# Two experts side by side on the column halves of TensorE, with plain transposes, one scatter for both, and second-layer weights loaded two rows to a packet

## The chip, the cores and the metric

The kernel runs on one core of one Trainium2 chip. The metric is the device time of one execution in microseconds, as the median of several runs. Everything is computed in float32; the dense products outside the experts split each operand into two parts, the expert products don't.

## What is computed

The reference is one block with retention, dilated attention and a mixture of experts, followed by a second block of two layers, all for 256 tokens of width 1024. The change touches the mixture of experts alone. Each token goes to 4 of 32 experts; an expert is two matrix products with a clamped SwiGLU between them:

```python
logits = (xf @ w_router + b_router)
top_val, top_idx = lax.top_k(logits, TOP_K)
gates = jax.nn.softmax(top_val, axis=-1)
...
u = xb @ w1[e] + b1[e]                       # w1[e]: 1024 x 2048
glu = jnp.minimum(u[:, ::2], SWIGLU_LIMIT)
lin = jnp.clip(u[:, 1::2], -SWIGLU_LIMIT, SWIGLU_LIMIT)
a = glu * jax.nn.sigmoid(SWIGLU_ALPHA * glu) * (lin + 1.0)
return a @ w2[e] + b2[e]                     # w2[e]: 1024 x 1024
...
y = y.at[row_tok].add(yb * row_gate[:, None])
```

## The kernel before

**The program.** First come the dense layers of the first block, then the router (lines 868 to 940), then the experts (to line 1160), then the second block. The expert stage lasts from some 369 to 1375 us of the profiled execution, half of the whole.

**Tokens in slots.** Each expert has 64 slots. `gather` (L965) picks the tokens of four experts at a time with one-hot matrices and leaves them transposed in the tile `hg`: hidden dimension on the partitions, 64 slots per expert along the free axis. Experts with more than 64 tokens are made up for in `past_slots`, a branch that is skipped when there are none.

**First product, `chunk(e)`.** The tokens are the stationary operand (128 rows, 64 columns), the weights stream through as 512 columns. 64 columns fill half of the array, so two products run beside each other, on its two column halves, into partitions 0 to 63 and 64 to 127 of one PSUM bank (`halves`, L995). Before the change the two halves are the odd and the even blocks of 128 hidden rows of the same expert: each half holds half of the sum. Each float32 product shows as two instructions in the trace.

**Merge and transpose.** The four banks are copied to `us` by ScalarE and VectorE (L320, L1014). Then 16 products per expert (L1019) with `jh`, two identity matrices of 64 on top of each other, add the two halves and transpose them in one step; the columns are read with a step of two, so that the two interleaved parts, gated and linear, come apart. Bias, clamp, activation and the last product follow on VectorE and ScalarE (L1022 to L1027) into `apk`.

**Second product, `second(e)`.** It runs the same way (L995 again, into banks of tag b), with the halves as even and odd blocks of the middle dimension. The result `ys` therefore again holds half sums in its two halves. For each pair of experts the scatter (L1059) multiplies by `spread`, a matrix with the gate of each token at its slot, twice, so that the halves are added on the way, and VectorE adds the result to `acc` (L1064). `spread_pair` builds two such matrices per token block and pair (L985, L987).

**Order of the work.** `jobs` puts the first product of expert e + 1 ahead of the second product of expert e, so that the activation of e is covered. A scheduler may move instructions within that.

**Weights.** `W.plan` is one list of tiles of 1 MB in the order of use; they are issued on SP's queue in that order (`load_next`, L143). During the expert stage they lie in two rings of six buffers, `raw` and `more`, which take turns in blocks of six; the first 16 tiles are loaded ahead, four of them into other buffers. A load waits until the tile that had its buffer has been used. A first-layer tile is 128 rows of 8 KB, one to a partition. A second-layer tile is 256 rows of 4 KB: partition p gets the rows p and p + 128, two packets of 4 KB. From 16 tiles before the end of the stage on, only the ring `raw` is used, and the tiles of the second block follow in it; those are split into two parts by ScalarE and VectorE (L172, L173).

Of the kernel before, what the change touches and what calls it, by code (L numbers as in the profile page):

```python
# [36 lines left out]
def constants():  # L37
# [5 lines left out]
    c["halves"] = np.concatenate([np.eye(64), np.eye(64)], axis=0)  # L43
    c["before"] = (i[:, None] < i[None, :])
    c["slots"] = np.tile(np.arange(64) + 1, (P, 2))
# [162 lines left out]
def body(tc, A, out, offs, dbg):  # L208
# [75 lines left out]
    jobs = [("c", 0)] + [j for e in range(31) for j in (("c", e + 1), ("h", e))] + [("h", 31)]  # L284
    for kind, e in jobs:
        for k in range(0, 8, 1 if kind == "c" else 2):
            W.add((kind, e, k), kpf(w1[e], 0, 2 * D, k, 1) if kind == "c" else kpf(w2[e], 0, D, k, 2), True)
# [659 lines left out]
    apk = pe.tile([P, 2, 8, SLOTS], F32, name="apk")  # L947
    b1T = pe.tile([P, 2, 8, 32], F32, name="b1T")
    us_ = pa.tile([P, 4, 512], F32, name="us", tag="x1")
    jh = con("halves")  # L950
    spread, ys = {}, {}
# [20 lines left out]
    for g in range(2):  # L972
        for k in range(8):
            f0 = k % 4 * 256 + g
            PE.transpose(b[:, (g * 8 + k) * 32:(g * 8 + k + 1) * 32], b1w[k // 4][:, f0:f0 + 255:2], ident[:32, :32])
    copy_s(b1T.rearrange("p g k e -> p (g k e)"), b)

    def spread_pair(p_):

        od = pe.tile([P, 2, 2, P], F32, name="od")  # L980
        b = bank("b").rearrange("p (e b t) -> p e b t", e=2, b=2)
        for i in range(2):
            for tb in range(2):
# [4 lines left out]
        spread[p_] = pe.tile([P, 2, 2, P], F32, name="spread")  # L988
        copy_s(spread[p_], b)
# [7 lines left out]
    lo_, hi_ = slice(0, SLOTS), slice(SLOTS, P)  # L997

    def chunk(e, ahead):
        u = [bank("a") for _ in range(4)]  # L1000
        last = []
        for k in range(0, 8, 2):
            for g, d in ahead[k // 2:k // 2 + 1]:
# [6 lines left out]
        eb = [bank("b").rearrange("p (k s) -> p k s", k=8) for _ in range(2)]  # L1010
        us = us_ if e == 0 else pa.tile([P, 4, 512], F32, name="us", tag="x1")
# [540 lines left out]
```

## Time and profile before

| | us |
|---|---|
| median of 3 runs (2001.44 to 2003.26) | 2002.59 |
| the profiled execution | 2001.25 |
| its span, first to last instruction | 1999.3 |
| TensorE busy in the span | 1961.2 (98%) |
| VectorE busy | 819.3 (41%) |
| ScalarE busy | 597.2 (30%) |
| transfers on SP's queue | 583.07 MB, 76.7% of 16 engines' span |

Engines: PE is TensorE's products, PEld its weight loads, DVE is VectorE, ACT ScalarE, SP the queue that issues the loads. Where a row of windows lists busy times without names, they stand in the order PE, PEld, DVE, ACT, POOL. "Granted clock" is the share of TensorE's full clock. A matmul's end is modelled, so the busy share of TensorE is an upper bound, and what ends the waits of others tells more. The transfer share is the mean busy share of the 16 transfer engines. Bank tags a and b are two sets of four PSUM banks.

### The profile page before, as it was taken

To read this page: it belongs to the slowest core of one execution; us is meant where nothing else is said; L and a number is where in the kernel's file an instruction comes from. 1 tells how busy PE (TensorE), PEld (TensorE's weight loads), DVE (VectorE), ACT (ScalarE), POOL (GpSimd) and SP (SyncE) were. 2 spreads that over 40 slices of the span, in tenths; PEclk is the share of its full clock that TensorE was granted. 3 is DMA by queue.
4 is the path that set the end of the run, shared out by engine and by line. 5 is a ranking of instruction groups with operands and counts; after the bars stand their busy time and mean duration, and the time that the engine had idled before them with its cause. 6 is when DMAs were issued, how large, how long until landed. Compare 5 with 4: busy or idle time off the path is not lost. (4 is left out here: it accounts for less than half of the span.)

```text
span 1999.3 us, 25851 instructions
## 1 busy us (share of the span) xinstructions
PE 1961.2 (98%) x10812; PEld 1279.2 (64%) x10812; DVE 819.3 (41%) x1324; ACT 597.2 (30%) x900; POOL 2.6 (0%) x7
## 2 busy tenths in 40 slices
PE   7999999899999999999999999999999999999998
PEld 6899987544444444444444443436879998979997
DVE  6687577311211112121121111325665446556455
ACT  4535543211111111111111111103634444645443
POOL 0000000000000000000000000000000000000000
PEclk9999999999999999999999999999999999999999
DMA  9777576898999999999999999989536555336550
GB/s 361 258 245 235 179 265 243 325 394 333 414 386 400 417 379 416 396 402 418 382 416 391 404 417 382 376 351 375 198 127 211 188 180 181 126 105 207 180 183 22
DMA packets 203293, 593.26 MB, mean 297 GB/s; under 512 B 10587, under 2 KB 95158, under 8 KB 170402
## 3 DMA queue, kind: packets, MB, share of 16 engines
q1 hardware_dynamic: 196792, 583.07, 76.7%
q10 hardware_dynamic: 6378, 8.47, 1.3%
q8 instruction: 87, 1.43, 0.3%
q14 instruction: 36, 0.29, 0.0%
HBM read 590.44 MB, written 1.07 MB: 296 GB/s over the span
## 5 line engine op out<-in xcount | busy, mean ns | idle before, releaser
L173 DVE TENSOR_TENSOR wlo<-raw,whi 128x1024 fp32r<-128x1024 f32 x286 | 345.3, 1221 | 248.7 <-ACT whi L172 246.7
L172 ACT ACTIVATE whi<-raw 128x1024 fp32r<-128x1024 f32 x286 | 298.1, 1058 | 340.6 <-issue 101.9
L995 PE MATMUL bank_a<-more,hg 128*64 128x512 f32 x1440 | 318.5, 594 | 0.0
L995 PE MATMUL bank_b<-raw,apk 128*64 128x512 f32 x1024 | 264.7, 601 | 0.0
L995 PEld LDWEIGHTS bank_a<-more,hg 128*64 128x64 f32 x1440 | 101.7, 137 | 193.5 <-issue 190.7
L1014 DVE COPY us<-bank_a 128x512 f32<-128x512 f32 x64 | 44.2, 692 | 396.4 <-PE bank_a L995 396.4
L366 PE MATMUL bank_b<-xh,whi 128*128 128x256 f32 x640 | 181.2, 283 | 0.0
L368 PE MATMUL bank_b<-xh,wlo 128*128 128x256 f32 x640 | 181.0, 283 | 0.0
L367 PE MATMUL bank_b<-xl,whi 128*128 128x256 f32 x640 | 181.0, 283 | 0.0
L1019 PEld LDWEIGHTS bank_b<-cm,us 128*128 128x128 f32 x1024 | 127.0, 196 | 68.1 <-issue 41.4
L995 PEld LDWEIGHTS bank_b<-raw,apk 128*64 128x64 f32 x1024 | 70.0, 136 | 118.7 <-issue 97.6
L995 PE MATMUL bank_a<-raw,hg 128*64 128x512 f32 x608 | 141.8, 597 | 0.1
L1019 PE MATMUL bank_b<-cm,us 128*128 128x64 f32 x1024 | 138.4, 285 | 0.7 <-ACT us L320 0.7
L320 ACT ACTIVATE us<-bank_a 128x512 f32<-128x512 f32 x64 | 38.1, 597 | 289.0 <-PE bank_a L995 289.0
L366 PEld LDWEIGHTS bank_b<-xh,whi 128*128 128x128 f32 x640 | 122.7, 192 | 0.7
L367 PEld LDWEIGHTS bank_b<-xl,whi 128*128 128x128 f32 x640 | 122.6, 192 | 0.7
L368 PEld LDWEIGHTS bank_b<-xh,wlo 128*128 128x128 f32 x640 | 122.7, 192 | 0.0
L1059 PE MATMUL bank_b<-y,spread 128*128 128x512 f32 x256 | 122.4, 611 | 0.0
L995 PEld LDWEIGHTS bank_a<-raw,hg 128*64 128x64 f32 x608 | 42.2, 136 | 84.9 <-issue 77.2
L1059 PEld LDWEIGHTS bank_b<-y,spread 128*128 128x128 f32 x256 | 44.8, 189 | 76.7 <-issue 55.0
L1024 ACT ACTIVATE glu<-glu 128x512 f32<-128x512 f32 x32 | 20.2, 630 | 243.0 <-DVE glu L1023 243.0
L1064 DVE TENSOR_TENSOR acc<-bank_b,acc 128x512 f32<-128x512 f32 x52 | 36.0, 692 | 134.1 <-PE bank_b L1059 134.1
(389 smaller groups left out, 2896.2 us busy)
## 6 DMA issues: line engine op xcount, KB each, us to landing
raw<-in_w_mlp SPq DMA_DIRECT2D x204, 1024.0 KB, 10.4
more<-in_w_mlp SPq DMA_DIRECT2D x180, 1024.0 KB, 11.1
raw<-in_w_ffn_in SPq DMA_DIRECT2D x44, 1024.0 KB, 5.2
raw<-in_w_in SPq DMA_DIRECT2D x38, 1024.0 KB, 7.8
raw<-in_w_ada SPq DMA_DIRECT2D x24, 1024.0 KB, 7.6
raw<-in_w_ffn_out SPq DMA_DIRECT2D x22, 1024.0 KB, 5.0
raw<-in_b_w_in SPq DMA_DIRECT2D x10, 1024.0 KB, 5.2
raw<-in_w_mix_out SPq DMA_DIRECT2D x8, 1024.0 KB, 6.0
```

The costliest lines, as they stand in the source:

```text
L172: self.nc.scalar.activation(hi, w, AF.Copy)
L173: self.nc.vector.tensor_tensor(lo, w, hi.bitcast(F32), OP.subtract)
L320: return S.activation(o, i, AF.Copy, **kw)
L366: PE.matmul(v[:, m], hi[:, k, ms], xh[:, k], start=k == 0, stop=False)
L367: PE.matmul(v[:, m], hi[:, k, ms], xl[:, k], start=False, stop=False)
L368: PE.matmul(v[:, m], lo[:, k, ms], xh[:, k], start=False, stop=k == 7)
L995: last[:] = [PE.matmul(out[at], st, w, start=start, stop=stop)]
L1014: V.tensor_copy(us[:, c], u[c])
L1019: PE.matmul(eb[g][:, c * 2 + q], us[:, c, q * 256 + g:(q + 1) * 256:2], jh, start=True, stop=True)
L1024: S.activation(glu, glu, AF.Gelu_apprx_sigmoid)
L1059: PE.matmul(b, spread[e // 2][:, i, tb], ys[e - 1 + i][:, qs], start=i == 0 and e > 1, stop=i == 1)
L1064: v_ = V.tensor_tensor(to[:, tb, qs], b, to[:, tb, qs], OP.add)
```

## The change

It does the following:
- The two column halves of the array now belong to two experts of a pair p_, 2 p_ and 2 p_ + 1, for both products. Each half holds a whole sum over eight blocks.
- With whole sums nothing has to be added, so the 32 products of a pair with `jh` become 16 plain transposes of 128 x 128 (both experts at once). The hidden units are taken in another order: columns 4 m + 2 i + g of each block of 512 go to block k = 2 c + i, so that partition p of two neighbouring blocks holds two neighbouring units.
- Second-layer tiles follow that order: partition p gets rows 2 p and 2 p + 1, which lie next to each other in memory.
- One scatter matrix holds the slots of both experts, so the scatter is one product per bank and pair instead of two.
- Jobs, weight tiles and the calls of `gather` go by pairs: 16 first-layer tiles, then 8 second-layer tiles. The number and the sizes of the tiles, 384 of 1 MB, stay.
- `glu` and `lin` become one tile with the tag `retl`; the ring `more` is closed after the last first product.

The core of the diff:

```diff
@@ constants
-    c["halves"] = np.concatenate([np.eye(64), np.eye(64)], axis=0)
...
@@ weights
-    jobs = [("c", 0)] + [j for e in range(31) for j in (("c", e + 1), ("h", e))] + [("h", 31)]
+    jobs = [("c", 0)] + [j for p_ in range(15) for j in (("c", p_ + 1), ("h", p_))] + [("h", 15)]
...
-            W.add((kind, e, k), kpf(w1[e], 0, 2 * D, k, 1) if kind == "c" else kpf(w2[e], 0, D, k, 2), True)
+            for e in (2 * p_, 2 * p_ + 1):
+                ap = kpf(w1[e], 0, 2 * D, k, 1) if kind == "c" else \
+                    w2[e][k * P:(k + 2) * P].rearrange("(p k) f -> p k f", k=2)
+                W.add((kind, e, k), ap, True)
...
@@ spread_pair
-                V.tensor_scalar(od[:, i, tb], con("slots"), R[:, tb, e:e + 1], G[:, tb, e:e + 1], OP.is_equal,
-                                OP.mult)
-                PE.transpose(b[:, i, tb], od[:, i, tb], ident)
+                V.tensor_scalar(od[:, tb, i * SLOTS:(i + 1) * SLOTS], con("slots")[:, :SLOTS], R[:, tb, e:e + 1],
+                                G[:, tb, e:e + 1], OP.is_equal, OP.mult)
+            PE.transpose(b[:, tb], od[:, tb], ident)
...
@@ chunk
-        for k in range(0, 8, 2):
...
-            w = W.take_wholes(("c", e, k), ("c", e, k + 1))
+        for k in range(8):
...
+            w = W.take_wholes(("c", 2 * p_, k), ("c", 2 * p_ + 1, k))
             for c in range(4):
                 cs_ = slice(c * 512, c * 512 + 512)
-                halves(u[c], last, [(rows_, hg[e // 4][:, e % 4, k + i], w[i][:, 0, cs_], k == 0, k == 6)
-                                    for i, rows_ in ((1, hi_), (0, lo_))])
...
+                halves(u[c], last, [(rows_of[i], hg[p_ // 2][:, 2 * p_ % 4 + i, k], w[i][:, 0, cs_], k == 0, k == 7)
+                                    for i in range(2)])
...
+            b = bank("b").rearrange("p (g k s) -> p g k s", g=2, k=2)
             for g in range(2):
-                for q in range(2):
-                    PE.matmul(eb[g][:, c * 2 + q], us[:, c, q * 256 + g:(q + 1) * 256:2], jh, start=True, stop=True)
...
+                for i in range(2):
+                    f0 = 2 * i + g
+                    PE.transpose(b[:, g, i], us[:, c, f0:f0 + 509:4], ident)
+            ks = slice(2 * c, 2 * c + 2)
+            for g in range(2):
+                V.tensor_tensor(gl[:, g, ks].rearrange("p k (e s) -> p k e s", e=2),
...
@@ second
-                for i in range(2):
-                    PE.matmul(b, spread[e // 2][:, i, tb], ys[e - 1 + i][:, qs], start=i == 0 and e > 1, stop=i == 1)
+                PE.matmul(b, spread[p_][:, tb], y[:, qs], start=p_ > 0, stop=True)
```

How the instructions move, first on TensorE, for one pair without a gather in the middle of the stage. Before (a product counts once here; L995 into bank a is the first, into bank b the second layer):

```order
L995 MATMUL bank_a<-raw,hg_5210 64x512 x8
L995 MATMUL bank_a<-more,hg_5210 64x512 x24
L1019 MATMUL bank_b<-cm,us 128x64 x4
L995 MATMUL bank_b<-raw,apk 64x512 x4
L1019 MATMUL bank_b<-cm,us 128x64 x12
L995 MATMUL bank_b<-raw,apk 64x512 x8
L1059 MATMUL bank_b<-y,spread 128x512
L995 MATMUL bank_b<-raw,apk 64x512 x4
L1059 MATMUL bank_b<-y,spread 128x512 x4
L995 MATMUL bank_a<-raw,hg_5210 64x512 x8
L1059 MATMUL bank_b<-y,spread 128x512 x3
L987 MATMUL bank_b<-cm,od 128x128 x4
```

That is one expert's worth of products; the other expert of the pair has the same without the scatter. After, the whole pair:

```order
L996 MATMUL bank_a<-raw,hg_3975 64x512 x16
L996 MATMUL bank_a<-more,hg_3975 64x512 x24
L996 MATMUL bank_a<-raw,hg_3975 64x512 x16
L1024 MATMUL bank_b<-cm,us 128x128 x16
L996 MATMUL bank_b<-raw,apk 64x512 x8
L996 MATMUL bank_b<-more,apk 64x512 x24
L1061 MATMUL bank_b<-y,spread 128x512
L996 MATMUL bank_a<-raw,hg_3975 64x512
L1061 MATMUL bank_b<-y,spread 128x512 x3
L996 MATMUL bank_a<-raw,hg_3975 64x512 x7
L988 MATMUL bank_b<-cm,od 128x128 x2
```

The first products of a pair stand together (64 with the eight that lie around the scatter), its 16 transposes follow in one piece, then the 32 second products of the pair before. Next SP's queue, at the end of the stage, from the branch of `past_slots` on. Before:

```order
L1122 DMA mem<-in_mem 128x2x1024
L143 DMA raw<-in_w_mlp 128x2048 x2
L143 DMA more<-in_w_mlp 128x2048 x6
L143 DMA raw<-in_w_mlp 128x2x1024 x4
L143 DMA raw<-in_w_mlp 128x2048 x8
L143 DMA raw<-in_w_mlp 128x2x1024 x6
L1162 DMA gfin<-in_g_final 128x1024
L143 DMA raw<-in_w_mlp 128x2x1024 x2
L143 DMA raw<-in_w_mem_kv 128x8x256
```

After:

```order
L1124 DMA mem<-in_mem 128x2x1024
L142 DMA raw<-in_w_mlp 128x2048 x10
L1159 DMA gfin<-in_g_final 128x1024
L142 DMA raw<-in_w_mlp 128x2048 x10
L142 DMA raw<-in_w_mem_kv 128x8x256
```

All expert tiles are now one run of 2048 elements to a partition, those of the second layer too (2x1024 before). Eight more tiles are issued ahead of the branch, and ten instead of two behind `gfin`.

## Rows read from the trace of the kernel before

**Rows 1.** Page, busy tenths in 40 slices of the whole span (some 50 us each).

```profile
PE   7999999899999999999999999999999999999998
...
DMA  9777576898999999999999999989536555336550
```

**Rows 2.** Windows: length, busy us (instructions) per engine, granted clock, transfer share, GB/s.

```profile
600.00:1100.00 500.00, 500.00 (x2330) 211.24 (x2328) 97.80 (x184) 64.35 (x119) 0.00 (x0) 1.00 1.00 402
376.50:1375.50 999.00, 996.79 (x4630) 420.47 (x4627) 202.15 (x368) 127.71 (x231) 0.00 (x0) 1.00 0.97 392
```

**Rows 3.** Waits, 600 to 1100 us: who for whom, us in total, times, longest.

```profile
PEld bank_b L1019 <- ACT us L320: 13.0, 16, 0.8
PEld bank_b L995 <- DMA more<-in_w_mlp: 8.5, 18, 0.8
...
PEld bank_a L995 <- DMA raw<-in_w_mlp: 3.0, 4, 0.8
...
SPq L143 <- PE bank_a L995: 239.7, 64, 8.5
SPq L143 <- PE bank_b L995: 177.9, 64, 6.3
```

**Rows 4.** Timeline of TensorE: start us, us, line, output<-inputs, instructions.

```profile
601.13 2.10 PE L1019 MATMUL bank_b<-cm,us 128*128 128x64 f32 x16
...
660.53 2.10 PE L1019 MATMUL bank_b<-cm,us 128*128 128x64 f32 x16
...
726.56 2.10 PE L1019 MATMUL bank_b<-cm,us 128*128 128x64 f32 x16
```

**Rows 5.** Groups by line, 600 to 1100 us: instructions, busy us, mean ns, idle before.

```profile
L1019 PE MATMUL bank_b<-cm,us 128*128 128x64 f32 x512 | 69.7, 286 | 0.0
...
L1059 PE MATMUL bank_b<-y,spread 128*128 128x512 f32 x128 | 61.3, 612 | 0.0
...
L1014 DVE COPY us<-bank_a 128x512 f32<-128x512 f32 x32 | 22.1, 692 | 201.3 <-PE bank_a L995 201.3
...
L987 PE MATMUL bank_b<-cm,od 128*128 128x128 f32 x32 | 5.0, 279 | 0.0
```

**Rows 6.** Timeline of TensorE, the stage's last products, last scatter, next transposes.

```profile
1364.98 5.37 PE L995 MATMUL bank_b<-raw,apk 128*64 128x512 f32 x24
1370.29 5.42 PE L1059 MATMUL bank_b<-y,spread 128*128 128x512 f32 x12
1375.54 2.00 PE L529 MATMUL bank_b<-cm,mem 128*128 128x128 f32 x16
```

**Rows 7.** Windows of 20 us without a stop of the transfers.

```profile
620.00:640.00 20.00, 20.00 (x101) 8.70 (x98) 4.03 (x7) 2.65 (x5) 0.00 (x0) 1.00 1.02 420
680.00:700.00 20.00, 20.00 (x98) 8.66 (x96) 4.03 (x7) 1.82 (x3) 0.00 (x0) 1.00 1.02 419
```

**Rows 8.** Transfers in 4 us, second-layer tiles (704 to 708), first-layer tiles (504 to 508).

```profile
DMA packets 428, 1.64 MB, mean 410 GB/s; under 512 B 28, under 2 KB 28, under 8 KB 428
...
DMA packets 238, 1.70 MB, mean 424 GB/s; under 512 B 31, under 2 KB 31, under 8 KB 31
```

**Rows 9.** Windows of 1 us where the first buffers come back.

```profile
376.00:377.00 1.00, 1.00 (x8) 0.40 (x6) 0.00 (x0) 0.00 (x0) 0.00 (x0) 1.00 0.51 49
...
378.00:379.00 1.00, 1.00 (x8) 0.31 (x6) 0.00 (x0) 0.00 (x0) 0.00 (x0) 1.00 0.99 406
```

**Rows 10.** Timeline of the issuing queue, then of ScalarE: the next stage's first weights.

```profile
1359.74 0.37 SPq L143 DMA_DIRECT2D raw<-in_w_mem_kv  x1
...
1371.59 2.00 ACT L172 ACTIVATE whi<-raw 128x1024 fp32r<-128x1024 f32 x2 [14.41 <-DMA raw<-in_w_mem_kv]
```

**Rows 11.** Windows in the router (1 us each) and in the last stage.

```profile
362.00:363.00 1.00, 0.28 (x3) 0.21 (x4) 0.93 (x6) 0.00 (x0) 0.00 (x0) 0.50 1.04 434
...
366.00:367.00 1.00, 1.00 (x7) 1.00 (x6) 0.00 (x0) 0.38 (x1) 0.00 (x0) 0.50 1.05 434
...
1796.00:1808.00 12.00, 9.70 (x69) 8.02 (x68) 10.91 (x27) 5.03 (x8) 0.00 (x0) 1.00 0.22 78
```

More of the change, by code (lines that the diff above doesn't have):

```diff
@@ L946, in body @@
     acc = pa.tile([P, 2, D], F32, name="acc", tag="reth")
-    apk = pe.tile([P, 2, 8, SLOTS], F32, name="apk")
+    apk = pe.tile([P, 2, 8, P], F32, name="apk")
     b1T = pe.tile([P, 2, 8, 32], F32, name="b1T")
     us_ = pa.tile([P, 4, 512], F32, name="us", tag="x1")
-    jh = con("halves")
-    spread, ys = {}, {}
+    spread = {}
     def gather(g, d):
@@ L973, in body @@
         for k in range(8):
[L974 to L975 removed]
+            f0 = k % 4 // 2 * 512 + k % 2 * 2 + g
+            PE.transpose(b[:, (g * 8 + k) * 32:(g * 8 + k + 1) * 32], b1w[k // 4][:, f0:f0 + 509:4], ident[:32, :32])
     copy_s(b1T.rearrange("p g k e -> p (g k e)"), b)
     def spread_pair(p_):
[L980 to L983 removed]
+        od = pe.tile([P, 2, P], F32, name="od")
+        b = bank("b")[:, :T].rearrange("p (b t) -> p b t", b=2)
+        for tb in range(2):
+            for i in range(2):
                 e = 2 * p_ + i
[L985 to L988 removed]
+                V.tensor_scalar(od[:, tb, i * SLOTS:(i + 1) * SLOTS], con("slots")[:, :SLOTS], R[:, tb, e:e + 1],
+                                G[:, tb, e:e + 1], OP.is_equal, OP.mult)
+            PE.transpose(b[:, tb], od[:, tb], ident)
+        spread[p_] = pe.tile([P, 2, P], F32, name="spread")
         copy_s(spread[p_], b)
@@ L1032, in second @@
         for k in range(0, 8, 2):
-            w, = W.take_wholes(("h", e, k))
-            for h in range(2):
-                hs = slice(h * 512, h * 512 + 512)
-                halves(yb[h], last, [(rows_, apk[:, e % 2, k + i], w[:, i, hs], k == 0, k == 6)
-                                     for i, rows_ in ((0, lo_), (1, hi_))])
-        if e % 2 == 0:
-            both = pa.tile([P, 2, D], F32, name="y", tag="x2")
-            ys[e], ys[e + 1] = both[:, 0], both[:, 1]
+            w = W.take_wholes(("h", 2 * p_, k), ("h", 2 * p_ + 1, k))
+            for j in range(2):
+                for h in range(2):
+                    hs = slice(h * 512, h * 512 + 512)
+                    halves(yb[h], last, [(rows_of[i], apk[:, p_ % 2, k + j, rows_of[i]], w[i][:, j, hs],
+                                          k + j == 0, k + j == 7) for i in range(2)])
+        y = pa.tile([P, D], F32, name="y", tag="x2")
         for h in range(2):
             hs = slice(h * 512, h * 512 + 512)
-            if e < 28:
-                copy_s(ys[e][:, hs], yb[h])
-            else:
-                y_ = V.tensor_tensor(ys[e][:, hs], yb[h], gtf[:, hs], OP.mult)
-        if e == 31:
+            if p_ < 14:
+                copy_s(y[:, hs], yb[h])
+            else:
+                y_ = V.tensor_tensor(y[:, hs], yb[h], gtf[:, hs], OP.mult)
+        if p_ == 15:
             with after(y_):
                 W.split_to(2)
-        if e % 2 == 0:
-            return
         for tb in range(2):
@@ L1136, in mem_v @@
         copy_s(vm[i], gemm_v(("mv", i), *mem_parts))
-    ahead = {}
-    for g in range(1, 8):
-        for d in range(8):
-            ahead.setdefault(4 * g - 2 + d // 4, []).append((g, d))
-    for kind, e in jobs:
+    for kind, p_ in jobs:
         if kind == "c":
-            if e % 2:
-                spread_pair(e // 2)
-            chunk(e, ahead.get(e, ()))
-        else:
-            with W.urgent() if e == 31 else ExitStack():
-                last_x = second(e)
-        if (kind, e) == ("h", 27):
+            spread_pair(p_)
+            chunk(p_, [((p_ + 1) // 2, d) for d in range(8)] if p_ % 2 and p_ < 15 else [])
+        else:
+            with W.urgent() if p_ == 15 else ExitStack():
+                last_x = second(p_)
+        if (kind, p_) == ("h", 13):
             past_slots()
```

41 lines of the change are left out of this document (20 added, 21 removed).

## The prediction

> **What bounds the kernel now.** Read the busy shares by slices first: over the whole expert stage, slices 8 to 27, TensorE and the transfer engines both stand at nine tenths or more [rows 1]. The windows then show how near to each other the two are: from 600 to 1100 us TensorE is busy for all of 500 us at full granted clock, and the transfers are at a share of 1.00 with 402 GB/s; over the whole stage the mean is 0.97 and 392 GB/s [rows 2]. The view of waits says which of the two waits for the other. In those 500 us the weight loads of TensorE waited 11.5 us for transfers in all, none longer than 0.8 us, while the queue that issues the loads waited 417.6 us for TensorE to give a buffer back [rows 3]. So the buffers are mostly full and TensorE sets the pace; the transfers run close behind it, and stop for a moment when all buffers are full.
>
> The pace of a pair of experts: the same group of L1019 starts at 601.13 and, two pairs later, at 726.56 [rows 4], so 62.7 us a pair, and 16 pairs are 1003 us. A pair reads 24 tiles of 1.0486 MB, 25.17 MB; in 62.7 us that is 401 GB/s, which is the rate of the window.
>
> **What TensorE loses.** In the window of 500 us lie 8 pairs. Per pair and from the groups by line [rows 5]:
> - The merging transposes, L1019, are 64 instructions, 69.7 / 8 = 8.7 us. In their place stand 16 plain transposes of 128x128. A transpose is one instruction where a product is two, and 16 of them are seen at the end of this stage in 2.00 us [rows 6]. Their source is read here in steps of four elements instead of next to each other, which no row prices; the bounds are 2.0 us and the 8.7 us of L1019, which reads in steps of two. I take 2.0, since L987, plain transposes too, has 5.0 us for 32. Saved: 6.7 us.
> - The scatter, L1059, goes from 16 instructions to 8: 61.3 / 8 = 7.7 us becomes 3.8. Saved: 3.9 us.
> - The spread matrices, L987, go from four transposes to two: 0.6 becomes 0.3 us.
> - The two large products (L995) keep their number of instructions, 128 and 64 a pair, and their partition in column halves. Nothing.
>
> Together 10.9 us of 62.7, so TensorE needs some 52 us a pair. What the change puts after the products costs little: the evacuation copies of L1014 (0.69 us) and ScalarE's stood ahead of L1019 already; the bias additions are now eight short ones a pair instead of four long ones, over the same elements, on a VectorE that is busy for 97.8 of 500 us [rows 2]. The chain through the activation to the packed activations is hidden as before, behind the product of the pair before (32 products, 64 instructions). If that cover went, it would cost about 3 us a pair, still inside the slack below.
>
> **What is late next: the transfers.** 25.17 MB in 52 us would be 484 GB/s. When nothing stops them, the transfers do 420 and 419 GB/s in 20 us [rows 7]. So TensorE's saving, 16 times 10.9 = 174 us, can't come out whole: the stage will run at the rate of the transfers, and about 8 us a pair become waiting of TensorE for tiles.
>
> The rate depends on the packet. In a stretch with second-layer tiles alone (428 packets, all under 8 KB: two rows of 4 KB to a partition) it is 410 GB/s, in one of first-layer tiles (8 KB packets) 424 [rows 8]. The change lays the second layer out so that a partition's two rows follow each other in memory, one packet of 8 KB. I take 419 GB/s for the whole stream, the lower of the two 20 us windows, and 410 and 424 as its bounds. The gain from the packets alone is small: 8.39 MB a pair at 424 instead of 410 is 0.7 us, 11 us in all, and only because the transfers now bound.
>
> **The sum.** The start is not moved: the first 16 tiles are loaded before, the transfers stand still until the first buffers come back, and are at full rate from about 377.5 us [rows 9]. From there are left 368 tiles, 385.9 MB, the memory input (1.05 MB) and the final gain (0.5 MB), which the queue issues before the last tiles, and some 0.7 MB of instructions: 388.2 MB. At 419 GB/s that takes 926.5 us, to 1304.0 us. After the last tile come 16 instructions (24 take 5.37 us, so 3.6), one product on VectorE (0.7) and the last scatter (12 take 5.42 us, so 8 take 3.6) [rows 5, 6]: 1311.9 us. In the kernel before the same point, the first transpose of the memory input, is at 1375.54 [rows 6]. Gained: 63.6 us.
>
> The stage behind it keeps its length, I think. Today its first weights are issued at 1359.74 and are split no earlier than 1371.59, ScalarE having waited for them, 4 us before the stage ends [rows 10]: already now they come just in time, behind other transfers. With the change they land some 3 us behind the last expert tile, about 1307, again 5 us ahead. Behind it the transfers are busy for three to six tenths [rows 1], so they soon run ahead again. If this cover goes, the price is the landing of two or three tiles, up to 8 us.
>
> The profiled execution took 2001.25 us (its span 1999.3), 1.3 us under the median of 2002.59. 2001.25 - 63.6 = 1937.6, and on the median's scale **1939 us**.
>
> The Trainium skill (DMA: Bandwidth & Descriptors, Specifications) gives a limit of about 358 GB/s from HBM per core and a ceiling of 435 GB/s of the fabric. The trace disagrees with the first, as it has 402 GB/s over 500 us, and the measurement decides; by the second the same bytes would take 892 us, an estimate from that page, and the kernel about 1905 us; no run here shows such a rate.
>
> **Rivals.**
> - *TensorE stays the bound.* If the transposes with their wide steps cost what L1019 cost (8.7 us) and the serial start of 16 transposes adds 2 us of waiting for evacuation, a pair takes 52 + 6.7 + 2 = 60.7 us, just over the 60.1 us of the transfers. 16 times 2.0 us saved is 32: 1971 us. For it: L1019's weight loads waited for ScalarE's evacuation 16 times, up to 0.8 us [rows 3], and all 16 transposes of a pair now stand in one piece behind it. Against: L987 and the end of the stage show cheap transposes. Chance 0.12.
> - *The transfers don't get better than their present mean.* If 402 GB/s is what a queue that is never empty holds for long, because the 16 engines drift apart and the slowest decides, 388.2 MB take 965.7 us: 1978 us. For it: 20 us windows are short. Against: the stops in the mean are seen as waits for buffers [rows 3]. Chance 0.10.
> - *Slower: the granted clock.* The change makes TensorE wait for tiles about 8 us a pair. The trace shows the clock at its lower level: after some microseconds with short bursts in the router, 0.28 us busy out of 1, the granted clock is 0.50, so 1.2 GHz, and stays so while TensorE is busy all the time [rows 11]. If the waits for tiles did this in a share f of the time, a pair took 52 / (1 - f/2) us: hidden up to f = 0.27, slower than before from f = 0.34, at one half 69.3 us a pair and 2108 us. Against: with 9.70 of 12 us busy in the last stage the clock stayed at 1.00 [rows 11], and the expected waits are 8 of 60 us, in pieces of some 1.4 us (two tiles take 5.0 us to land and keep TensorE busy for 3.6); a slow stretch fills the buffers and ends the waits. Chance 0.05. The Trainium skill (TensorE: Matmul & The Clock Gate, HAM oscillation) tells of a kernel whose every burst began at the lower clock after a wait for a transfer; by that rule this rival would hold in full, and the row with 9.70 of 12 us speaks against it here.
> - *Nothing happens.* Were the packets unchanged and the transfers already at their limit over the whole stage, the time would stay at 2002. The list of issues speaks against it: every second-layer tile is now one run of 2048 elements to a partition. Chance 0.03.
>
> **How the numbers follow.** The forecast has 0.70. With 424 GB/s (915.6 us) it gives 1928, with 410 (946.8 us) 1959, with 8 us lost behind the stage up to 1967. The range from 1925 to 1975 holds these and the first rival, and leaves out most of the second and the others. A measurement of this kernel can tell about 0.2%, 4 us. Faster: the forecast and the first two rivals, 0.92, and a part of the clock rival, where the slow share stays small, 0.02; within 0.2%: 0.03; slower: 0.03.
>
> **What would show it.** Right: in the windows of the stage a share near 1.00 without dips, 415 to 424 GB/s, all packets 8 KB; the waits of the issuing queue for TensorE gone and in their place waits of the weight loads for transfers, 100 us or more in all; 60 us from pair to pair; the stage's end near 1312. The transposes in 2 to 3 us a pair, the scatter in under 4. Wrong: TensorE's waits for transfers still near 11 us (it bounds), a rate of 402 with no waits of the issuing queue, a granted clock of 0.50 inside the stage, or the first split after it late by more than 8 us.

## The result, and the profile after

The changed kernel takes 1953.24 us (median of 4 runs, 1951.99 to 1956.18) against 2002.25 us for the kernel before on the same chip: a ratio of 0.9757, 95% interval 0.974 to 0.9774. The gain is 49.0 us; the prediction had 63.6 us, 1939 us and a range of 1925 to 1975. The profiled execution took 1951.99 us, its span 1949.9 us, 49.4 us less than the span before.

In the page, TensorE's row and the transfers' row have changed places: TensorE now falls to eight tenths in many slices of the expert stage and the transfers stand at nine tenths [rows 1]; the rate stands still at 419 to 420 GB/s. There are two dips in it, in slice 8 (385) and in slice 25 (365; the slices count from 0).

```profile
PE   7999999899998989989899898789999999999998
...
DMA  9777587799999999999999999898545555326550
GB/s 360 267 241 242 175 270 275 288 385 420 419 420 420 420 419 419 419 420 419 420 420 419 419 420 419 365 414 287 172 157 189 178 190 194 109 87 217 193 173 22
```

The windows, with the columns of [rows 2]: in the middle TensorE is busy for 453.76 of 500 us, at full granted clock, and the transfers do 420 GB/s where they did 402. The other rows are the whole stage, its start, and the place of the dip in slice 25.

```profile
376.50:1322.00 945.50, 867.33 (x3708) 327.71 (x3704) 172.06 (x344) 86.20 (x155) 0.00 (x0) 1.00 1.00 414
...
377.50:400.00 22.50, 22.50 (x108) 7.46 (x104) 0.69 (x1) 1.00 (x2) 0.00 (x0) 1.00 1.00 406
400.00:420.00 20.00, 20.00 (x92) 8.20 (x92) 7.03 (x16) 4.07 (x7) 0.00 (x0) 1.00 0.93 353
600.00:1100.00 500.00, 453.76 (x1946) 175.82 (x1942) 91.61 (x189) 45.14 (x83) 0.00 (x0) 1.00 1.01 420
1230.00:1260.00 30.00, 24.90 (x97) 8.28 (x98) 7.40 (x8) 0.98 (x2) 0.00 (x0) 0.89 0.83 329
```

The waits of 600 to 1100 us have turned round. The issuing queue waited 417.6 us for TensorE [rows 3]; now it waits 412.1 us for transfers, and TensorE's weight loads wait for tiles, 89.3 us in three rows.

```profile
PEld bank_b L996 <- DMA more<-in_w_mlp: 39.8, 39, 2.2
PEld bank_a L996 <- DMA raw<-in_w_mlp: 25.9, 22, 2.2
PEld bank_a L996 <- DMA more<-in_w_mlp: 23.6, 18, 3.8
...
SPq L142 <- DMA raw<-in_w_mlp: 211.8, 100, 3.7
SPq L142 <- DMA more<-in_w_mlp: 200.3, 98, 3.6
SPq L142 <- PE bank_a L996: 17.3, 31, 2.7
```

TensorE's timeline: from the transposes of one pair to those of the next it is 59.85 us, where [rows 4] had 62.7. The 16 transposes take 2.40 us; the scatter, L1061, takes 4 us in its two pieces. The last rows are the end of the stage and answer to [rows 6].

```profile
603.28 3.65 PE L996 MATMUL bank_a<-raw,hg 128*64 128x512 f32 x14 [1.34 <-DMA raw<-in_w_mlp]
606.86 2.40 PE L1024 MATMUL bank_b<-cm,us 128*128 128x128 f32 x16
...
626.80 1.13 PE L1061 MATMUL bank_b<-y,spread 128*128 128x512 f32 x2
...
628.86 2.84 PE L1061 MATMUL bank_b<-y,spread 128*128 128x512 f32 x6
...
666.71 2.40 PE L1024 MATMUL bank_b<-cm,us 128*128 128x128 f32 x16
...
1314.00 3.65 PE L996 MATMUL bank_b<-raw,apk 128*64 128x512 f32 x14 [1.38 <-DMA raw<-in_w_mlp]
...
1317.66 3.67 PE L1061 MATMUL bank_b<-y,spread 128*128 128x512 f32 x8
...
1321.17 1.04 PE L531 MATMUL bank_b<-cm,mem 128*128 128x128 f32 x8
...
1322.99 0.39 PE L368 MATMUL bank_a<-mem_h,whi 128*128 128x256 f32 x1 [0.78 <-ACT mem_h L322]
```

So the mechanism is the one forecast, and 14.2 us of the gain are missing. The first transpose of the memory input is at 1321.17 and not at 1311.9: 9.3 us. From there to the end of the span it is 628.7 us, where before it was 1999.3 - 1375.54 = 623.8: 4.9 us more. The first part is in the windows. Against 419 GB/s from 377.5 us on, 22.5 us at 406 lose 0.7 us, 20 us at 353 lose 3.2, and 30 us at 329 lose 6.4. The 500 us in the middle ran at 419.6 (209.81 MB); over the 810 us from 420 to 1230 that gives 1.2 us back. Together it is 9.1 of the 9.3 us. The last of the three losses is at the branch for experts with more than 64 tokens (`past_slots`), where the issuing queue stands still for 19.9 us:

```profile
1226.40 10.29 SPq L142 DMA_DIRECT2D more<-in_w_mlp  x5
1256.59 0.39 SPq L1124 DMA_DIRECT2D mem<-in_mem  x1
1257.09 18.48 SPq L142 DMA_DIRECT2D raw<-in_w_mlp  x10
```

The built program says why. Loads take eight semaphores in turn (DMAHW0 to DMAHW7), so each load waits for the eighth before it. Where SyncE passes the branch it waits for all eight, since the skipped body has loads of its own on that queue. In this list of SyncE's instructions, each has beside it the waits that stand ahead of it; the trace shows the eight waits, the last at 1256.4 us:

```
563 L1081 UNCONDITIONAL_BRANCH [waits DMAHW0_49,DMAHW1_49,DMAHW2_49,DMAHW3_49,DMAHW4_49,DMAHW5_49,DMAHW6_49,DMAHW7_49]
564 L1124 DMA mem<-in_mem 128x2x1024 [waits DVE_49,DMAHW0_49,PE_49,Activation_49]
565 L142 DMA raw<-in_w_mlp 128x2048 [waits DMAHW1_49,PE_49]
```

```profile
L1081 SPq EVENT_SEMAPHORE  x8: 17/17/17, 1243.8 to 1256.4; - x8
```

In the kernel before, the queue waited at the same place (first row, 1255 to 1290 us), but no wait of TensorE for a tile follows until 1330 us. In the changed kernel TensorE itself stops for 5.1 us at the branch, and behind that stop the granted clock is at 0.50 (second row):

```profile
SPq L1079 <- SPq L1079: 14.0, 5, 5.3
```

```profile
1240.00:1242.00 2.00, 2.00 (x8) 0.51 (x6) 0.00 (x0) 0.00 (x0) 0.00 (x0) 0.50 1.01 410
```

### The profile page after: what moved, and what is told of

It reads as the page before. It is cut to its first block, busy times and chain, and to the rows that moved or that the text cites. A ratio compares the mean times of both kernels' runs of the same rounds, so it can differ in the third digit from the quotient of the medians.

```text
span 1949.9 us, 23889 instructions
## 1 busy us (share of the span) xinstructions
PE 1834.2 (94%) x9884; PEld 1188.6 (61%) x9884; DVE 790.3 (41%) x1304; ACT 555.7 (28%) x824; POOL 2.6 (0%) x7
## 5 line engine op out<-in xcount | busy, mean ns | idle before, releaser
L996 PE MATMUL bank_a<-raw,hg 128*64 128x512 f32 x1280 | 334.0, 606 | 21.0 <-DMA raw<-in_w_mlp 20.7
L996 PEld LDWEIGHTS bank_a<-raw,hg 128*64 128x64 f32 x1280 | 97.1, 138 | 214.1 <-issue 167.9
L996 PE MATMUL bank_a<-more,hg 128*64 128x512 f32 x768 | 177.8, 595 | 18.2 <-DMA more<-in_w_mlp 18.2
L996 PE MATMUL bank_b<-more,apk 128*64 128x512 f32 x672 | 163.1, 597 | 29.5 <-DMA more<-in_w_mlp 29.5
L368 PE MATMUL bank_b<-xh,whi 128*128 128x256 f32 x640 | 181.2, 283 | 0.0
L996 PEld LDWEIGHTS bank_b<-more,apk 128*64 128x64 f32 x672 | 60.0, 136 | 128.9 <-issue 59.5
L996 PEld LDWEIGHTS bank_a<-more,hg 128*64 128x64 f32 x768 | 60.1, 137 | 125.5 <-issue 90.1
L368 PEld LDWEIGHTS bank_b<-xh,whi 128*128 128x128 f32 x640 | 122.7, 192 | 0.7
L996 PE MATMUL bank_b<-raw,apk 128*64 128x512 f32 x352 | 83.3, 598 | 4.4 <-DMA raw<-in_w_mlp 4.2
L1474 PE MATMUL bank_a<-wlo,ah 128*128 128x512 f32 x176 | 69.8, 396 | 0.0
L1475 PE MATMUL bank_a<-whi,al 128*128 128x512 f32 x176 | 69.7, 396 | 0.0
L1473 PE MATMUL bank_a<-whi,ah 128*128 128x512 f32 x176 | 69.7, 396 | 0.0
## 6 DMA issues: line engine op xcount, KB each, us to landing
raw<-in_w_mlp SPq DMA_DIRECT2D x204, 1024.0 KB, 19.9
more<-in_w_mlp SPq DMA_DIRECT2D x180, 1024.0 KB, 19.9
```

Source lines behind the costliest of these rows:

```text
L368: PE.matmul(v[:, m], hi[:, k, ms], xh[:, k], start=k == 0, stop=False)
L996: last[:] = [PE.matmul(out[at], st, w, start=start, stop=stop)]
L1473: PE.matmul(ops[tb, h], ah[:, k, ts], hi[:, k, hs], start=n + k == 0, stop=False)
L1474: PE.matmul(ops[tb, h], ah[:, k, ts], lo[:, k, hs], start=False, stop=False)
L1475: PE.matmul(ops[tb, h], al[:, k, ts], hi[:, k, hs], start=False, stop=n + k == 11)
```

## The experiments

Four questions: does the transfer really bound, and how far off is TensorE; what are the packets worth, with the change and without it; what are the three losses (branch, start, stage behind); and does mending them add up. The router's end lies between 361.5 and 367.4 us in these profiles, for something ahead of the stage that I did not look into, so places in the stage are compared from there. The length of the stage is taken from the router's end to the first product of the memory keys (L368): 961.5 us in the changed kernel, 961.8 in a second profile of it. Ratios are against the kernel before, timed on the same chip.

### How far off is TensorE? Half of the second layer's loads left out

```diff
-            for e in (2 * p_, 2 * p_ + 1):
+            for e in (2 * p_, 2 * p_ + 1) if kind == "c" or k < 4 else ():
...
-            w = W.take_wholes(("h", 2 * p_, k), ("h", 2 * p_ + 1, k))
+            if k < 4:
+                w = W.take_wholes(("h", 2 * p_, k), ("h", 2 * p_ + 1, k))
```

and the end of the ring `more` moves with the number of tiles, from 368 to 304.

> The changed kernel with half of the second-layer loads left out: hidden slices 4 to 7 are multiplied by the weights of slices 2 and 3 again (that half of the second layer is not computed). TensorE's work is the same, the transfers fall from 24 to 20 tiles a pair, 20.97 MB, 49.9 us at 420 GB/s. It measures TensorE's own pace. Theory by the trace of the changed kernel (TensorE busy 453.8 of 500 us, 54.4 us of a 59.9 us pair): a pair takes 54 to 55 us, TensorE hardly waits, 16 x 5 = about 80 us faster than the changed kernel. By the prediction's estimate of TensorE (52 us a pair): 16 x 8 = about 125 us faster. Rival (TensorE needs the 60 us itself): no faster.

Measured: 1847.04 us, ratio 0.9222 (0.9207 to 0.9236), 106 us below the changed kernel. TensorE is busy without a break (first row) and from the second of these rows to the third, six pairs later, it is 314.48 us, 52.4 us a pair (pairs with and without a gather alternate):

```profile
600.00:1100.00 500.00, 500.00 (x2232) 187.14 (x2234) 102.56 (x212) 52.04 (x97) 0.00 (x0) 1.00 0.98 400
```

```profile
599.86 2.40 PE L1024 MATMUL bank_b<-cm,us 128*128 128x128 f32 x16
...
914.34 2.40 PE L1024 MATMUL bank_b<-cm,us 128*128 128x128 f32 x16
```

The prediction's 52 us holds, and not the 54.4 that the expectation read off the busy share of the changed kernel, so that share holds some waiting too. Of 16 times 7.5 us, 120, 106 came out; the start, where TensorE is busy without a break until after 420 us in the changed kernel too, is one place with no slack to give.

### TensorE work put back

```diff
-                    PE.transpose(b[:, g, i], us[:, c, f0:f0 + 509:4], ident)
+                    for _ in range(2):
+                        PE.transpose(b[:, g, i], us[:, c, f0:f0 + 509:4], ident)
...
-                PE.matmul(b, spread[p_][:, tb], y[:, qs], start=p_ > 0, stop=True)
+                for _ in range(2 if p_ else 1):
+                    PE.matmul(b, spread[p_][:, tb], y[:, qs], start=p_ > 0, stop=True)
```

> The changed kernel with TensorE work put back: each of the 16 plain transposes of a pair is issued twice (16 more by 0.15 us, 2.4 us) and each of the 8 scatter matmuls twice from the second pair on (8 more by 0.5 us, 4.0 us), the second writing over the first, so 6.4 us more TensorE work for each of 16 pairs. Theory (transfers set the pace and TensorE waits about 46 of 500 us for them, 5.5 us in a pair): the work fills those waits, and only what is over them shows, 0 to 0.9 us a pair, 0 to 14 us in all. Rival (TensorE sets the pace): 16 times 6.4, about 102 us slower.

Measured: 1956.36 us, ratio 0.9783 (0.9768 to 0.9798), 3 us over the changed kernel by the medians and 5 by the ratios, whose intervals overlap, where the rival had 102. TensorE is busy for 494 of 500 us and the rate is still 420 GB/s; 52.4 + 6.4 = 58.8 us just fits under the 59.9 of the transfers. By the trace the stage is 4.9 us longer, 966.4.

```profile
600.00:1100.00 500.00, 494.38 (x2189) 196.40 (x2186) 94.54 (x189) 45.19 (x83) 0.00 (x0) 1.00 1.01 420
```

So the halved scatter was hardly needed for this time, nor was the last bit of the transposes; the transfers would bind without them.

### The packets undone

```diff
-                    w2[e][k * P:(k + 2) * P].rearrange("(p k) f -> p k f", k=2)
+                    kpf(w2[e], 0, D, k, 2)
...
-                    f0 = 2 * i + g
-                    PE.transpose(b[:, g, i], us[:, c, f0:f0 + 509:4], ident)
+                    f0 = 256 * i + g
+                    PE.transpose(b[:, g, i], us[:, c, f0:f0 + 255:2], ident)
```

> The changed kernel with the second-layer weights loaded as before, two 4 KB packets for each partition instead of one of 8 KB, and the transposes and the bias taken at the hidden units that belong to that order. The arithmetic is the same. Theory (transfers set the pace of the stage): 134.2 MB of the stage's 402.7 MB move at about 410 GB/s instead of 420, 134.2/410 - 134.2/420 = 7.8 us, so about 1961 us, and the windows of the second layer's loads show about 410 GB/s. Rival (TensorE still sets the pace, or the rate does not hang on the packets): within 2 us of the changed kernel.

Measured: 1962.0 us, ratio 0.981 (0.9795 to 0.9825), 9 us over the changed kernel by the medians and 11 by the ratios, whose intervals do not overlap; the theory had 7.8, and by the trace the stage is 7.3 us longer, 968.8. The rate in the middle falls to 416 GB/s, the mean of a stream with a third at 410; a stretch of second-layer tiles alone (616 to 620 us) shows that rate. The 16 transposes take 2.40 us with a step of two elements as well, so between steps of two and four there is no difference in this form; 16 transposes of contiguous columns are at 2.00 us [rows 6].

```profile
600.00:1100.00 500.00, 452.72 (x1936) 165.33 (x1932) 91.31 (x189) 45.19 (x83) 0.00 (x0) 1.00 1.02 416
```

```profile
DMA packets 429, 1.64 MB, mean 410 GB/s; under 512 B 29, under 2 KB 29, under 8 KB 429
```

### The packets alone, in the kernel before

```diff
-... kpf(w2[e], 0, D, k, 2), True)
+... w2[e][k * P:(k + 2) * P].rearrange("(p k) f -> p k f", k=2), True)
...
-                    PE.matmul(eb[g][:, c * 2 + q], us[:, c, q * 256 + g:(q + 1) * 256:2], jh, start=True, stop=True)
+                    PE.matmul(eb[g][:, c * 2 + q], us[:, c, 2 * q + g:2 * q + g + 509:4], jh, start=True, stop=True)
```

> The kernel before the change with one part of the change alone: the second-layer weights two rows to a packet (8 KB for each partition instead of two of 4 KB), with the transposing matmuls and the bias taken at the hidden units that belong to that order. Theory (TensorE sets the pace of the stage before the change, so faster transfers only wait for buffers): within 3 us of the kernel before. Rival (transfers set part of the pace already): up to 7.8 us faster, the price of 134.2 MB at 420 instead of 410 GB/s.

Both fell. Measured: 2176.36 us, ratio 1.0865 (1.0849 to 1.0882), 174 us slower than the kernel before. The packets ask for hidden units four columns apart. In the merging matmuls `us` is the stationary operand, and its load has become dearer: in the view of one line, durations as least, median and most in ns, the load takes 329 where it took 196 and the matmul 397 where it took 281 (the first two rows are the kernel before).

```profile
L1019 PE MATMUL bank_b<-cm,us x512: 281/281/333, 601.1 to 1071.8; 128*128 128x64 f32 x171
L1019 PEld LDWEIGHTS bank_b<-cm,us x512: 193/196/197, 601.1 to 1071.8; 128*128 128x128 f32 x171
```

```profile
L1019 PE MATMUL bank_b<-cm,us x446: 397/397/497, 599.7 to 1088.9; 128*128 128x64 f32 x149
L1019 PEld LDWEIGHTS bank_b<-cm,us x445: 307/329/332, 599.9 to 1088.8; 128*128 128x128 f32 x149
```

In the timeline 16 of them take 4 us where [rows 4] have 2.10, and behind the second of these groups, though not behind the first, the granted clock is at 0.50, 1.2 GHz, with no wait of TensorE in the rows:

```profile
708.28 3.94 PE L1019 MATMUL bank_b<-cm,us 128*128 128x64 f32 x16
...
741.00 4.00 PE L1019 MATMUL bank_b<-cm,us 128*128 128x64 f32 x16
```

```profile
744.00:748.00 4.00, 4.00 (x12) 2.27 (x12) 0.00 (x0) 0.00 (x0) 0.00 (x0) 0.50 1.02 424
...
600.00:1100.00 500.00, 500.00 (x2002) 236.77 (x2003) 86.44 (x161) 55.57 (x103) 0.00 (x0) 0.94 0.86 342
```

A pair has 64 of these matmuls: 4 x (3.94 - 2.10) = 7.4 us more, 118 us in 16 pairs. A mean clock of 0.94 over a stage of some 1170 us would take up to 70 us, where 56 are left; that is an estimate, no run here separates the two. So the packets and the plain transposes are one change: with plain transposes the step of four costs no more than one of two, in the old form it costs more than three times what the whole change gains. The Trainium skill (SBUF — State Buffer, Door 1, the note on 16-byte lines) says that an access which crosses to a new line pays, and that two hits a line are wanted, and also that four float32 can be strided for free. A step of four float32 is one hit per 16 bytes, a step of two is two. The trace agrees with the first for these loads, 329 ns against 196, and not with the second; and the transposes, which read the same columns, show no difference between the two steps.

### The branch

```diff
-                            nc.sync.dma_start(w, w1e[es_, :, k0:k0 + 4, m * 256:(m + 1) * 256]...)
+                            nc.gpsimd.dma_start(w, w1e[es_, :, k0:k0 + 4, m * 256:(m + 1) * 256]...)
```

and the same for the body's two other loads; the second kernel has no branch at all.

> The changed kernel with one thing moved: the loads inside the branch for experts with more than 64 tokens are issued by GpSimd instead of SyncE, so that SyncE, which issues all weight loads, no longer waits at the branch's end for its eight loads under way. Theory (the stop of 19.9 us without a load at the branch costs the transfers about 6.3 us, 20 us at 287 instead of 419 GB/s, and nothing hides it): 5 to 8 us faster, and the window at the branch stays near 419 GB/s. Rival (the stop is that of the branch itself on every engine, or the cover of the buffers makes it up later): within 2 us of the changed kernel.

> The changed kernel without the branch and its body: the tokens over 64 of an expert are not made up for (that part of the computation is left out). Theory (all that the branch costs is SyncE's stop): the same gain as moving the branch's loads to GpSimd, 5 to 8 us. Rival (the branch also costs what the other engines stop for, 5.1 us on TensorE and a stretch at half clock): 3 us or more beyond the kernel with GpSimd's loads.

Measured: 1948.78 us, ratio 0.9742 (0.9724 to 0.976) with GpSimd's loads, and 1946.43 us, 0.9733 (0.9719 to 0.9746) without a branch. The hole is gone, 416 GB/s with GpSimd's loads (first row; the trace has no waits of SyncE at L1081 any more) and 420 without a branch (second row), where there were 329:

```profile
1230.00:1260.00 30.00, 24.92 (x98) 8.20 (x96) 7.39 (x8) 1.58 (x3) 0.00 (x0) 0.94 1.01 416
```

```profile
1230.00:1260.00 30.00, 27.32 (x106) 9.43 (x106) 7.30 (x8) 1.58 (x3) 0.00 (x0) 1.00 1.01 420
...
1308.00:1312.00 4.00, 4.00 (x22) 1.29 (x18) 0.00 (x0) 0.00 (x0) 0.00 (x0) 1.00 0.49 168
```

So the cause of the hole is shown. What it is worth is less clear. With GpSimd's loads the stage is 957.3 us long, 4.2 less than in the changed kernel, of the 6.4 in the hole; by the times it is 3 to 4.5 us, short of the 5 to 8 expected, and the intervals overlap with the changed kernel's. Without a branch the times give 5 to 7 us, the intervals overlap too, and the profile, of the slowest of the five executions (1958.26 us, the others 1945.36 to 1951.49), has a stage of 962.5 us: nothing is gained there. The hole comes back behind the place: the last 20 loads, which have only one ring of six buffers, show dips, 301 GB/s at 1272 us, 350 at 1300 and 168 at 1308 (third row). In this one execution it is what the first rival's second half says. The times of the two kernels can't be told apart, so nothing shows that the stop of TensorE at the branch costs anything of its own.

### The start and the memory rows

The start, with the bias transposes made a function:

```diff
-        for d in range(8):
+        for d in range(3):
             gather(0, d)
...
+            if p_ == 0 and k == 3:
+                bias_t()
+                spread_pair(0)
             w = W.take_wholes(("c", 2 * p_, k), ("c", 2 * p_ + 1, k))
...
-            spread_pair(p_)
-            chunk(p_, [((p_ + 1) // 2, d) for d in range(8)] if p_ % 2 and p_ < 15 else [])
+            if p_:
+                spread_pair(p_)
+            first = [(0, d) for d in range(3, 8)] if p_ == 0 else []
+            chunk(p_, [((p_ + 1) // 2, d) for d in range(8)] if p_ % 2 and p_ < 15 else first)
```

The memory rows:

```diff
             past_slots()
+            mem_load()
...
             gfin = pa.tile([P, 2048], F32, name="gfin", tag="x1")[:, :D]
-            mem_load()
+            mem_t()
...
-    mem_t()
     kmT, vm = [], []
```

> The changed kernel with TensorE's order at the start of the expert stage changed: the transposes of the bias, the first pair's spread and five of the eight gathers of the first group are placed between the first steps of the first layer instead of ahead of the last matmuls of step 0, which hold the first two buffers. The arithmetic is the same. Theory (transfers stand still from about 370 to 377 us only because the first two buffers come free 5 us late, and the stage behind is bound by transfers): transfers start 4 to 5 us earlier and the end comes 3 to 5 us earlier. Rival (the issuing queue waits for TensorE again at 400 to 420 us, where it is still behind): the gain is given back there, 0 to 1 us.

> The changed kernel with the transposes and splits of the memory rows moved from behind the expert stage to before its last half pair, where TensorE waits for transfers; the load of the memory rows is asked for at the end of pair 13 instead of pair 14. The arithmetic is the same. Theory (behind the stage TensorE waits for the splits of the memory rows, and that stretch is 4.9 us longer than before the change, 628.7 against 623.8 us): 3 to 5 us faster, the first matmul of the memory keys follows the last scatter at once. Rival (the memory keys' weights, which land about 4 us before, or the norm of x set that place): within 1 us of the changed kernel.

Measured: 1950.72 us, ratio 0.9736 (0.9723 to 0.975), for the start, and 1949.19 us, 0.9736 (0.9721 to 0.9752), for the memory rows. By the times the first gains 2.5 to 4 us and the second 4, with intervals that overlap the changed kernel's. The traces say less. At the start the first load goes out at 371.71 instead of 375.20, 5.0 us earlier when counted from the router's end, but six loads later the queue waits for the other ring, and there is a hole that was not there before:

```profile
371.71 9.31 SPq L142 DMA_DIRECT2D raw<-in_w_mlp  x6
391.12 7.67 SPq L142 DMA_DIRECT2D more<-in_w_mlp  x6
```

```profile
388.00:392.00 4.00, 4.00 (x22) 1.37 (x20) 0.32 (x1) 0.00 (x0) 0.00 (x0) 1.00 0.09 37
```

The stage is 960.7 us long, 0.8 less than in the changed kernel: the rival's price. For more than that the two profiles give no place that the edit touched. With the memory rows moved the stage is 960.4 us long, 1.1 less. Their products do follow the last scatter at once, but now TensorE waits at the next place, for ScalarE's split of x:

```profile
1319.51 3.70 PE L1061 MATMUL bank_b<-y,spread 128*128 128x512 f32 x8
1322.64 0.68 PE L368 MATMUL bank_a<-mem_h,whi 128*128 128x256 f32 x1
...
1331.93 0.50 PE L334 MATMUL bank_a<-whi,xh 128*128 128x512 f32 x1 [2.10 <-ACT xh L322]
```

From the first product of the memory keys to the end of the span it was 621.3 us before the change, 626.9 after, and 624.7 here. The 2.2 us can't be put down to the rows, though: the kernel with GpSimd's loads, whose rows are in their old place, has 624.5, the one with the start's order 625.0, the one with TensorE's work put back 624.4. What these share with the moved rows is the granted clock, 1.00 in the 15 us behind the first product where the changed kernel has 0.89 (in order: changed kernel, rows moved, GpSimd's loads):

```profile
1323.00:1338.00 15.00, 12.67 (x76) 11.22 (x77) 14.72 (x31) 10.16 (x14) 1.85 (x2) 0.89 1.11 344
```

```profile
1323.00:1338.00 15.00, 12.49 (x81) 10.28 (x80) 12.38 (x28) 10.75 (x16) 1.75 (x2) 1.00 1.10 345
```

```profile
1323.00:1338.00 15.00, 12.47 (x86) 11.00 (x87) 14.72 (x32) 10.47 (x16) 1.85 (x2) 1.00 1.10 344
```

Three more profiles with the rows in their old place have 0.89 there (the packets undone, no branch, the changed kernel a second time), and 626.3 to 626.9 us. The changed kernel has another such stretch from 1398 to 1413 us, 0.89 too, and the kernel with the rows moved has none. So about 2 of the 5.6 us go with stretches at the lower clock. Whether one comes does not hang on the rows alone: the last kernel below has the rows moved and 0.89. What the other 3.4 us are is open.

### All of it together

The last three kernels ran on one chip with the changed kernel, which took 1954.89 us there, ratio 0.9762 (0.9748 to 0.9777). First the three edits above. Then also another order of the first 16 tiles (`load_at` is `load_next` for a given tile):

```diff
-    W.on_more = {first_b + i for i in range(8, 368) if (i < 14 if i < 16 else (i - 16) // 6 % 2)}
-    for i, tag in ((6, "x1"), (7, "x2")):
+    W.on_more = {first_b + i for i in range(6, 368) if (i < 12 if i < 16 else (i - 16) // 6 % 2)}
+    for i, tag in ((12, "x1"), (13, "x2")):
...
-    while W.loaded < first_b + 14:
-        W.load_next()
+    for i in (12, 13, 6, 7, 8, 9, 10, 11):
+        W.load_at(first_b + i)
+    W.loaded += 8
```

Then the second ring kept open longer: 376 in place of 368, and its end moved from behind the first product of pair 15 to behind the second product of pair 14.

> The changed kernel with three places mended at once: the branch's loads issued by GpSimd, the memory rows transposed before the last half pair, and the start's order on TensorE. The arithmetic is that of the changed kernel. Theory (the hole at the branch and the wait for the memory rows are losses of their own and add up; the start gives its gain back): 3 to 5 us from the branch, 3 to 5 from the memory rows, 0 to 2 from the start, 6 to 11 us below the changed kernel. Rival (they share one cover: once the branch's hole is gone, the last 20 loads, which have only the six buffers of one ring, set the end): no more than the best single one, about 4 us.

> The three places mended, and the order of the first 16 loads changed: the four buffers that are lent for the start only hold tiles 12 to 15 instead of 6, 7, 14 and 15, so that the second ring's six buffers come free from tile 6 on. The arithmetic is the same. Theory (the hole of 37 GB/s at 388 to 392 us in the kernel with the start's order changed is the wait for the second ring's first buffer): 2 to 4 us below the kernel with three places mended. Rival (TensorE, which is behind until about 410 us, sets the transfers there anyway): the hole moves to 400 to 412 us and the time stays within 1 us.

> All of that, and the second ring kept open for half a pair more, so that only the last 10 loads of the stage, not the last 20, go through the six buffers of the first ring alone. The arithmetic is the same. Theory (the last loads wait for TensorE to give back one of six buffers, 24 to 28 us of waits of the issuing queue behind the branch): 2 to 4 us below the kernel before it. Rival (those waits are hidden, six tiles of 2.5 us under way being enough): within 1 us.

Measured: 1948.03 us, ratio 0.9731 (0.9718 to 0.9744); 1946.12 us, 0.9726 (0.9712 to 0.974); 1944.09 us, 0.9712 (0.9698 to 0.9726). The three edits give 6.9 us by the times, less than their single gains added up, and the interval does not touch the changed kernel's. By the traces the stage is 956.4 us long, 5.4 less than the 961.8 of the changed kernel's profile on this chip, where the single traces gave 4.2 + 0.8 + 1.1. Behind the stage it is 626.3 us against 626.8, next to nothing. The order of the first tiles can't be told from nothing, and the trace has the rival's picture: the hole leaves 388 to 392 us, and 400 to 420 us falls to 265 GB/s. The longer ring can't be told from nothing by the times either, 2.0 us with overlapping intervals; in the trace 1260 to 1300 us go at 419 GB/s, where the kernel without it has 406, and the stage is 2.3 us shorter. All edits together are 10.8 us below the changed kernel, and the intervals do not touch; of that the stage has 7.1 us by the traces, 954.7 against 961.8. Behind this stage the clock is again 0.89 for 15 us, with the rows moved. What is left in the stage is above all the start, TensorE being busy in all of it:

```profile
400.00:420.00 20.00, 20.00 (x93) 7.64 (x89) 7.73 (x17) 4.69 (x7) 0.00 (x0) 1.00 0.75 288
1230.00:1260.00 30.00, 24.82 (x98) 8.11 (x96) 7.40 (x8) 1.58 (x3) 0.00 (x0) 0.94 1.01 416
```

## Why the prediction was right, and where it was off

- **The bound changes over: right.** TensorE needs 52.4 us a pair by the run with fewer loads, 52 by the prediction; the transfers make it 59.9, 60.1 by the prediction. Work of 6.4 us a pair put back on TensorE cost 3 to 5 us in all. The waits of the weight loads for tiles came to 89.3 us, a little under the 100 that were to show it.
- **The terms of TensorE:** the scatter 4.0 us against 3.8, the transposes 2.4 against 2.0. Both were hidden. The bounds of the transposes, 2.0 to 8.7 us, held, but "no row prices" the step of four was too mild: for the old form of L1019 it would have been 16 us a pair, which no bound held. It takes both, the step of four and the old form: the plain transposes cost the same with a step of two or of four.
- **The rate: right.** 419 GB/s was taken from 20 us and held for 500. The Trainium skill (DMA: Bandwidth & Descriptors, Specifications) has a limit of some 358 GB/s from HBM for a core and 435 for the fabric; the trace again disagrees with the first, 420 GB/s over 500 us, and stays under the second.
- **The packets: right in kind.** 11 us by the prediction, 7.8 by the expectation, 9 to 11 measured by the times and 7.3 by the trace of the stage.
- **The step that failed is the sum's "at 419 GB/s that takes 926.5 us", without a stop from 377.5 us to the last tile.** The stage has two stops: 3.9 us are lost between 377.5 and 420 us, where TensorE, busy all the time, gives buffers back too late (in the view of waits the queue waits for its first products for 58.6 us between 370 and 430 us), and 6.4 us at the branch. The second was in the trace before as well: the queue waits there for 14.0 us in the view of waits, and TensorE, which set the pace, shows no wait for a tile behind it. No term of the prediction speaks of the branch.
- **The other step is "the stage behind it keeps its length, I think".** It got 4.9 us longer, inside the 8 us that the text allowed for. The weights were split 4 us ahead of the stage's end, as before, so the cover that the text feared for did not go. What the profiles show instead are stretches of TensorE at half clock behind some short waits (1330 to 1334 us: 0.60), which go with about 2 of the 5.6 us counted from the first product of the memory keys. The rest is open.
- **The range** held the time, but in part by its width: its upper side was drawn for a rate of 410 GB/s, for a lost cover behind the stage and for TensorE as the bound, none of which came, and the stops that did come are in no term.
- **The rival of the clock:** TensorE waits for tiles in 46 of 500 us, in pieces of up to 2.9 us, and the granted clock is 1.00 in the whole window. In the stage's pace the rival did not come true; the sign "a granted clock of 0.50 inside the stage" did, behind the 5.1 us stop at the branch, without setting the time. The prediction applied the Trainium skill (TensorE: Matmul & The Clock Gate, HAM oscillation) too widely: the kernel told of there computed for less time than it waited for each transfer, and the same section has a larger case, where computing outlasts the waits, that stays at the full clock. The trace agrees with the latter: bursts of 3.65 us between waits of some 1.3.

## What to carry to other kernels

When a change moves the bound from an engine to the transfers, go through the stage for every place where the queue that issues the loads stops (a branch, a short ring, a late buffer): stops that were free before now have a price, here some 10 us of a forecast gain of 63.6. In this program a skipped branch with loads in its body drained the queue they are issued on, so such loads belong on a queue that nobody waits for; what that gives is known only when the places behind it (here a short ring) don't take it back. Reading an operand in steps of four instead of two cost nothing in one form of instruction and some 118 us in another, so a new memory order must be weighed with the instruction that will read it, not by itself. And a difference behind the edited place is to be compared over several kernels before it is put down to an edit: here the profiles of kernels that left that part alone spread over 2.5 us.

## What was not expected of the hardware

- The stationary operand of the old merging matmuls (float32, 128 x 128) loads in 329 ns when read in steps of four elements, in 196 ns in steps of two; transposes of the same columns take 2.40 us for 16 with either step, and 2.00 us for contiguous ones.
- With no wait in its rows, TensorE's granted clock still fell to 0.50 right behind one group of 16 matmuls with such loads, and not behind the group before it.
- 28,794 packets, 209.81 MB in 500 us, went at 420 GB/s, between 417 and 422 in each of 40 slices, with loads of 1 MB that took 19.9 us (median) from issue to landing: eight under way at a time, set by the program's semaphores, not by the twelve buffers.
